# Running a gated linear recurrence inside the attention loop instead of ahead of it

## The chip, the cores and the metric

One Trainium2 chip, all 8 cores; each core computes one element of a batch of 8. The metric is the device time of the slowest core in microseconds (us). Before the change the kernel took 5171.43 us (median of 4 runs, 5058.72 to 5303.1; the two of them in the fast state, explained next, took 5059 and 5064).

Runs come in two states. In the fast one all cores end within about 1% of each other. In the slow one the cores of one die, or a pair of them, show a lower granted clock for part of the run, and the time is some per cent longer. Only fast runs, or cores that were not slowed, are compared here. In the profile, PE is TensorE, PEld its weight loads, ACT ScalarE, DVE VectorE, POOL GpSimd, SP SyncE (SPq its queue of transfers).

## The reference

One layer of a hybrid backbone: 4096 latent tokens and 256 context tokens of width 1024. Two mixers read the same normalised input; a SwiGLU block follows. Cut to what matters:

```python
# mixer A: bidirectional gated linear recurrence, width 1280
r = sigmoid(blockdiag(xc) @ wa + ba);  i = sigmoid(blockdiag(xc) @ wx + bx)
log_a = -8 * r * softplus(-lam);       a = exp(log_a)
b = sqrt(-expm1(2 * log_a)) * (i * xc)
h = scan(a, b) forward + scan(a, b) backward
ya = (h * gelu(g)) @ w_out_lru
# mixer B: attention, 8 query heads, 2 key heads, head size 128, 4096 queries x 4352 keys
yb = softmax(q @ k.T / sqrt(128)) @ v @ w_out_attn
x = x + g_m * ((sigmoid(ga) * ya + sigmoid(gb) * yb) @ w_out)     # then x + g_f * swiglu(...)
```

Nothing in mixer A needs mixer B before the two are joined, so the two may run at once.

## The kernel before

Its stages are modulation, input projections (A), recurrence (B), attention with the output projections of each tile of 512 queries (C), feed-forward (D). B, with cuts marked:

```python
for m in range(10):                       # 128 channels each
    for d in range(2):                    # two directions
        ab, a2 = abuf[d], a2buf[d]        # two decay buffers of 128 x 4352
        for (c0, n) in wtiles:            # 256, then 4 x 1024 columns
            ...                           # gate products: 2 gates x 2 or 3 weight chunks
            act(trt, psum_a, AF.Tanh);  act(ab[:, c0:c0+n], trt, AF.Exp)
            tt("pool", a2[:, c0:c0+n], ab[...], ab[...], ALU.mult)
            act(ti[:, c0:c0+n], psum_x, AF.Tanh)
        act(a2, a2, AF.Sqrt, scale=-0.25, bias=0.25)      # one pass over 4352 columns
        stt(ti, ti, 1.0, x32, ALU.add, ALU.mult)
        tt("dve", a2, a2, ti, ALU.mult)
        scan(...)
```

and the loop of C, 8 tiles x 8 heads x 17 pairs of key blocks:

```python
emit_S(0); emit_S(1)                      # query-key products of two iterations ahead
for i in range(len(items)):
    emit_rest(i)                          # exp, then 4 products: 2 with V, 2 with ones (the denominators)
    if i + 2 < len(items): emit_S(i + 2)
# in emit_rest, at a head's end (pr == 16):
    recip(rd, pd); tt("dve", att[h], po, rd, ALU.mult)    # VectorE reads the denominators from PSUM
```

After each tile, C also makes its output projections and converts one eighth of the feed-forward weights to bf16 for D; the transfers and casts of that lie beside the attention.

## Time and profile before

| stage of a fast core | us |
|---|---|
| modulation and A | 1358 |
| B, recurrence | 742 |
| C, attention, output projections, weight conversion | 1922 |
| D, feed-forward | 1034 |

The table of busy time by stage and the timelines are shown in the prediction. Here are three groups of instructions of core 0, which ended as in a fast run; the columns are line, engine, operation, output and inputs, shape, count, then busy time and mean ns of one, then the engine's idle time just before them and what ended most of it.

```profile
L309 ACT ACTIVATE pt<-psq 128x1024 bf16<-128x1024 f32 x1088 | 1112.9, 1023 | 731.6 <-PE psq L312 731.3
L312 PE MATMUL psq<-pt,Vt 128*128 128x512 bf16 x2176 | 820.7, 377 | 9.6 <-ACT pt L309 8.1
L312 PE MATMUL psq<-xcb,gw 128*128 128x512 bf16 (+1 forms) x936 | 298.6, 488 | 406.1 <-ACT tib L309 167.1 <-POOL gw L341 149.5 <-ACT trt L309 62.7
```

The attention's exponentials on ScalarE leave 732 us in which ScalarE waits for TensorE, while TensorE's products with V wait 10 us: TensorE bounds C. In B TensorE waits 406 us ahead of its 299 us of gate products. This is what invites the change.

### The profile page before, as it was taken

The page shows a single profiled execution, that of the slowest core. Times are in us where ns is not written, and L with a number is a line of the kernel's source. Part 1 is how long each engine was busy: PE and PEld are TensorE (multiplying, and loading weights), DVE is VectorE, ACT ScalarE, POOL GpSimd, SP SyncE. Part 2 cuts the span into 40 slices and gives each one's busy share as a digit, 9 for nine tenths or more (in the row PEclk, how much of TensorE's full clock was granted, in tenths as well). Part 3 has the DMA queues.
Part 4 walks back from the last instruction along what each step waited for, and adds up shares of the span by engine and source line. Part 5 has one row for each costly group of instructions (what it writes and reads, how often), then busy time and mean ns, then how long its engine had stood idle before and what let it go on. Part 6 is the DMA issues. An engine that isn't in the chain of part 4 may idle for free.

```text
span 5277.8 us, 55043 instructions; the slowest of 8 cores (5055.7 to 5277.8 us)
## 1 busy us (share of the span) xinstructions
PE 4418.2 (84%) x18234; PEld 1935.7 (37%) x18234; DVE 1599.1 (30%) x1353; ACT 2424.5 (46%) x3049; POOL 1223.2 (23%) x788
## 2 busy tenths in 40 slices
PE   8778777778444442999999999999999899999999
PEld 8533333333111110333333333333343344444444
DVE  0244444444366776121212222121212111111111
ACT  0455555555466554747474655746363211111111
POOL 2133333333366664210102021110101000000000
PEclk9999898899666675999999999998887777787889
DMA  9522122222222221621203030221210411111011
GB/s 300 166 81 81 64 85 83 83 83 73 92 95 91 89 89 56 193 84 45 98 20 114 9 109 28 90 74 46 76 33 17 167 48 48 48 48 48 30 43 37
DMA packets 208453, 417.75 MB, mean 79 GB/s; under 512 B 18416, under 2 KB 123376, under 8 KB 199728
## 3 DMA queue, kind: packets, MB, share of 16 engines
q1 hardware_dynamic: 208176, 414.23, 23.2%
q8 instruction: 153, 2.51, 0.2%
q14 instruction: 124, 1.02, 0.1%
HBM read 279.28 MB, written 134.87 MB: 78 GB/s over the span
## 4 chain that ended last, share of the span: by engine, by line
PE 64%; POOL 9%; DMA 8%; ACT 8%; issue 5%; DVE 5%; SPq 1%; ACTq 0%; DVEq 0%; POOLq 0%
PE psq L312 62%; POOL a2buf L318 5%; DMA TBd<-to 2%; DMA TA<-to 2%; POOL gw L341 2%; DMA XC<-xco 2%; ACT abuf L309 1%; PE psq L315 1%; POOL g L318 1%; POOL t L318 1%; ACT a2buf L309 1%; ACT L309 1%; ACT trt L309 1%; DVE xco L327 1%; ACT tib L309 1%
## 5 line engine op out<-in xcount | busy, mean ns | idle before, releaser
L309 ACT ACTIVATE pt<-psq 128x1024 bf16<-128x1024 f32 x1088 | 1115.0, 1025 | 788.4 <-PE psq L312 788.2
L312 PE MATMUL psq<-pt,Vt 128*128 128x512 bf16 x2176 | 848.2, 390 | 8.8 <-ACT pt L309 7.5
L312 PE MATMUL psq<-pt,onesb 128*128 128x512 bf16 x2176 | 849.6, 390 | 0.0
L312 PE MATMUL psq<-hT,wi 128*128 128x512 bf16 (+1 forms) x3040 | 698.4, 388 | 129.5 <-ACT ub L309 94.4
L312 PE MATMUL psq<-hfT,wfi 128*128 128x512 bf16 x2816 | 717.5, 426 | 0.0
L312 PE MATMUL psq<-qt,KT 128*128 128x512 bf16 x2176 | 672.0, 392 | 13.9 <-DMA qt<-Q 11.0
L312 PE MATMUL psq<-xcb,gw 128*128 128x512 bf16 (+1 forms) x936 | 291.0, 477 | 425.2 <-ACT tib L309 174.5
L330 DVE RECIPROCAL rden<-psq 128x512 f32<-128x512 f32 x64 | 214.9, 3358 | 1322.0 <-PE psq L312 1322.0
L312 PEld LDWEIGHTS psq<-hT,wi 128*128 128x128 bf16 x3040 | 300.2, 100 | 531.5 <-issue 231.8
L312 PEld LDWEIGHTS psq<-hfT,wfi 128*128 128x128 bf16 x2816 | 300.9, 107 | 413.2 <-issue 354.8
L318 POOL TENSOR_TENSOR a2buf<-abuf 128x1024 f32<-128x1024 f32 (+1 forms) x100 | 348.7, 3487 | 238.8 <-ACT abuf L309 238.8
L312 PEld LDWEIGHTS psq<-pt,Vt 128*128 128x128 bf16 x2176 | 211.5, 97 | 522.3 <-issue 418.3
L309 ACT ACTIVATE sg<-psq 128x512 f32<-128x512 f32 x176 | 105.3, 598 | 573.5 <-PE psq L312 573.4
L318 POOL TENSOR_TENSOR mt<-tmpc,mB 128x512 bf16<-128x512 f32 x64 | 80.9, 1265 | 1238.5 <-DVE tmpc L327 1238.5
L312 PE MATMUL psq<-wfo,aT 128*128 128x512 bf16 x1408 | 356.0, 423 | 0.0
L318 POOL TENSOR_TENSOR x1l<-tmpd,x1l 128x512 f32<-128x512 f32 x64 | 81.2, 1269 | 1107.6 <-DVE tmpd L318 936.0
L312 PEld LDWEIGHTS psq<-xcb,gw 128*128 128x128 bf16 x936 | 104.2, 118 | 611.5 <-issue 563.2
L312 PEld LDWEIGHTS psq<-qt,KT 128*128 128x128 bf16 x2176 | 217.5, 100 | 290.8 <-issue 88.2
L318 DVE TENSOR_TENSOR aT<-sg,psq 128x512 bf16<-128x512 f32 x176 | 121.1, 688 | 659.1 <-PE psq L312 645.2
L327 DVE SCALAR_TENSOR_TENSOR xco<-ub,pp,xco 128x512 f32<-128x512 f32 (+3 forms) x270 | 198.4, 755 | 278.8 <-ACT ub L309 204.7
L312 PEld LDWEIGHTS psq<-pt,onesb 128*128 128x128 bf16 x2176 | 214.8, 99 | 155.6 <-issue 36.2
L312 PEld LDWEIGHTS psq<-wfo,aT 128*128 128x128 bf16 x1408 | 149.7, 106 | 205.0 <-issue 167.0
(101 smaller groups left out, 4430.5 us busy)
## 6 DMA issues: line engine op xcount, KB each, us to landing
wm<-w_mod SPq DMA_DIRECT2D x12, 2048.0 KB, 12.0
stg<-w_in SPq DMA_DIRECT2D x24, 1024.0 KB, 14.6
xc<-XC SPq DMA_DIRECT2D x10, 2176.0 KB, 12.3
stgc<-w_ffn_in SPq DMA_DIRECT2D x40, 512.0 KB, 4.2
xt<-x SPq DMA_DIRECT2D x32, 512.0 KB, 6.5
xtc<-x SPq DMA_DIRECT2D x32, 512.0 KB, 9.8
X<-xtc SPq DMA_DIRECT2D x32, 512.0 KB, 2.8
xs<-X SPq DMA_DIRECT2D x32, 512.0 KB, 5.3
```

The costliest lines, as they stand in the source:

```text
L309: return S.add("act", lambda e: e.activation(out=out, in_=in_, func=func, **kw), reads, writes)
L312: return S.add("pe", lambda e: e.matmul(out, lhsT=lhsT, rhs=rhs, start=start, stop=stop), reads, writes)
L315: return S.add("pe", lambda e: e.transpose(out=out, in_=in_, identity=ident), reads, writes)
L318: return S.add(eng, lambda e: e.tensor_tensor(out=out, in0=in0, in1=in1, op=op), reads, writes)
L327: return S.add("dve", lambda e: e.scalar_tensor_tensor(out=out, in0=in0, scalar=scalar, in1=in1, op0=op0, op1=op1), reads, writes)
L330: return S.add("dve", lambda e: e.reciprocal(out=out, in_=in_), reads, writes)
L341: return S.add(eng, lambda e: e.tensor_copy(out=out, in_=in_), reads, writes)
```

## The change

Its intent is to fill TensorE's and ScalarE's idle time. The recurrence becomes a Python generator that emits one small step (256 columns instead of 1024) at a time, and the attention loop takes a step every 2.3 iterations. The buffers of both have to fit together, so the decay buffers go from two to one, the gates get a single PSUM bank, and the denominators one instead of two. VectorE would hold that bank for a reciprocal of 3.36 us, so ScalarE now copies the denominators out first. The output projections and the weight conversion no longer fit and move to a stage of their own after the attention, which goes through a new DRAM buffer.

```diff
+        def lru_steps():
+            for m in range(10):
 ...
+                    for t_ in range(NT):                       # 17 steps of 256 columns
+                        for gate in range(2):
+                            for ki, k in enumerate(ks):
+                                mm(psG.t[:, gate * 256:(gate + 1) * 256], ...)
+                        def gate_acts(...):                    # emitted two iterations later
+                            act(trt, psG[0:256], AF.Tanh); act(ti, psG[256:512], AF.Tanh)
+                            act(ab, trt, AF.Exp); tt("pool", a2, ab, ab, ALU.mult)
+                        pend.append([it[0], gate_acts])
+                        yield
+                    stt(...); act(a2, a2, AF.Sqrt, ...)
+                    yield
+                    tt("dve", a2, a2, ti, ALU.mult)
+                    yield
+                    scan(...)
+                    yield
+                    yield
 ...
             for i in range(len(items)):
                 emit_rest(i)
                 if i + 2 < len(items): emit_S(i + 2)
+                lru_pump()                                     # 0.44 steps per iteration
 ...
-                    recip(rd, pd); tt("dve", att[h], po, rd, ALU.mult)
+                    act(pds, pd, AF.Copy)                      # ScalarE, out of PSUM
+                    recip(rdb, pds); tt("dve", ato, po, rdb, ALU.mult)
+                    dma("sp", AT_d[h, tile], ato)
 ...
+        # new stage: loads of AT, Z, gates, x; output projections; weight conversion
```

## The prediction

> **What bounds the kernel now.** I read the spans of the cores first. The profiled run is a slow one; cores 0, 1, 6 and 7 ended at 5056 to 5070 us, as the two fast timed runs (5058.7, 5063.5) did, while cores 2 to 5 took 5243 to 5278. So core 0 stands for a fast run here, and every number below is of core 0 unless I say otherwise. Then I read one table of busy time by stage: modulation (to 204), input projections A (to 1358), gated recurrence B (to 2100), attention with output projections C (to 4022), feed-forward D (to the end).
>
> ```profile
> core 0: us, PE busy (x) PEld busy (x) DVE busy (x) ACT busy (x) POOL busy (x), PEclk, DMA share, GB/s
> 204.00:1358.00 1154.00, 1015.83 (x3748) 441.50 (x3746) 508.52 (x623) 659.50 (x1229) 389.55 (x328) 0.77 0.23 80
> 1358.00:2100.00 742.00, 298.55 (x936) 106.62 (x936) 495.29 (x90) 415.49 (x359) 447.87 (x140) 0.64 0.23 83
> 2100.00:4022.00 1922.00, 1861.91 (x8208) 730.46 (x8208) 393.70 (x328) 1115.41 (x1091) 258.37 (x224) 0.99 0.22 73
> 4022.00:5056.00 1034.00, 978.44 (x4496) 458.46 (x4496) 197.58 (x288) 213.39 (x330) 81.61 (x64) 0.96 0.19 66
> ```
>
> In B nothing is full: PE is busy 299 of 742 us, and the chain of waits goes through GpSimd squares, weight casts and scans. In C PE is full and VectorE and GpSimd are nearly idle. The change runs B inside C's attention loop, to fill one with the other.
>
> How tight is that loop? The timeline of ScalarE in it:
>
> ```profile
> 2127.42 1.02 ACT L309 ACTIVATE pt<-psq 128x1024 bf16<-128x1024 f32 x1 [0.71 <-PE psq L312]
> 2128.72 1.02 ACT L309 ACTIVATE pt<-psq 128x1024 bf16<-128x1024 f32 x1 [0.27 <-PE psq L312]
> 2130.14 1.02 ACT L309 ACTIVATE pt<-psq 128x1024 bf16<-128x1024 f32 x1 [0.40 <-PE psq L312]
> 2131.44 1.02 ACT L309 ACTIVATE pt<-psq 128x1024 bf16<-128x1024 f32 x1 [0.27 <-PE psq L312]
> ```
>
> Two exponentials take 2.72 us, 1.36 an iteration. PE's six 512-column matmuls start 0.2158 us apart (57 of them take 12.46 us in the projection that follows, the last one 0.38), so they need 1.295. The loop keeps two score tiles in flight, so its period is a round trip over two iterations: exponential 1.02, hand-over to PE 0.15, six matmuls 1.295, drain and hand-back 0.25, together 2.72. PE has only 0.065 us of slack in an iteration; ScalarE, whose back-to-back exponentials start 0.93 apart, has 0.43.
>
> What the recurrence costs ScalarE shows in the timeline of B:
>
> ```profile
> 1399.02 1.09 ACT L309 ACTIVATE tib<-psq,lc 128x1024 f32<-128x1024 f32 x1
> 1401.23 1.28 ACT L309 ACT_TABLE_LOAD   x1 [1.11 <-POOL a2buf L318]
> 1402.52 3.83 ACT L309 ACTIVATE a2buf<-a2buf 128x4352 f32<-128x4352 f32 x1
> 1406.37 1.28 ACT L309 ACT_TABLE_LOAD   x1
> 1407.67 0.47 ACT L309 ACTIVATE trt<-psq,lc 128x256 f32<-128x256 f32 x1
> 1408.23 0.60 ACT L309 ACTIVATE abuf<-trt,lc 128x256 f32<-128x256 f32 x1
> 1408.74 0.45 ACT L309 ACTIVATE tib<-psq,lc 128x256 f32<-128x256 f32 x1
> ```
>
> The square root waits 1.1 us for GpSimd's last square, then takes a table load, 3.83 us and a load back: ScalarE does nothing else for 7.5 us.
>
> [...] 1.28 us, two loads at each square root, none between tanh and exp. So putting tanh beside the attention's exp is free of loads; the 20 square roots are not. [...] after 8 us of idle at the start of C,
>
> ```profile
> 2119.32 1.86 PE L312 MATMUL psq<-qt,KT 128*128 128x512 bf16 x4 [8.06 <-DMA qt<-Q]
> ...
> 2123.25 0.63 PE L312 MATMUL psq<-pt,onesb 128*128 128x512 bf16 x1
> 2123.68 0.63 PE L312 MATMUL psq<-pt,Vt 128*128 128x512 bf16 x1
> 2124.11 0.63 PE L312 MATMUL psq<-pt,onesb 128*128 128x512 bf16 x1
> ```
>
> matmuls start 0.43 us apart until 2126.2, then 0.216. [...] The cap is in the trace, 0.81[...]: cores 0 and 1 have it from 204 to about 1500 us and again from about 1600 to 1700, while cores 2 and 3 of the same die don't; they and cores 4 and 5 get it from 3590 to 3800 on, for about 1300 us, in the midst of dense work. That is the slow state. [...] With all eight cores running the trace shows 304 GB/s in the first 100 us at a DMA share of 0.97; I use 300.
>
> **The change, part by part.** Stages up to 1358 us and D (1034 us) are not touched. In place of B and C (2664 us) stand a fused stage and a projection stage.
>
> Fused stage. (a) Head: keys, values and the first queries are loaded as at the start of C now, where PE waited some 20 us: 22. (b) The loop alone: 8 tiles x 136 iterations x 1.36 = 1480. (c) Gate steps: 10 x 2 x 17 = 340 of 256 columns, one in every 2.3 iterations. On PE each is 2 gates x 2.6 weight chunks x 0.11 (half of 0.216) = 0.57 us, put between the scores and the next value matmuls. PE's slack is 0.065, so nearly all of it lengthens the round trip: 340 x 0.58 = 197, taking the slack as lost to ScalarE's uneven load. Its ScalarE work is two tanh and one exp, 0.47 + 0.45 + 0.60 less two overlaps of 0.09, 1.3 us every 2.3 iterations, against a slack there of 2.3 x 0.43 + 0.57 = 1.56: it fits on average, barely. (d) Square roots: 20 x 7.5 = 150, all on the path, since ScalarE runs in order and the next exponential stands behind. (e) PE is idle over 8 us at each, goes to half clock and comes back after 5 us, in which two iterations run instead of 3.7: 20 x 2.3 = 46. (f) The denominators now have one PSUM bank, and ScalarE copies it out at the end of each of 64 heads. That copy waits for the last ones-matmul, so the next exponential starts 1.86 us after the last one's end instead of 0.34. Part of these 1.5 us comes back from the slack: 64 x 1.1 = 70. (g) The pipeline drains at 8 tile ends: 10. (h) The cap still holds when the loop now starts at 1380: to 1500 and 1600 to 1700, 220 us at 0.81[...]: 25. Sum: 22 + 1480 + 197 + 150 + 46 + 70 + 10 + 25 = 2000.
>
> VectorE (495 us of recurrence, and 64 x (3.36 + 0.69) for the heads) and GpSimd (under 450) fit easily in 2000. The scheduling leaves four empty steps after a square root, about 24 us, for multiply, product and scan (5.4 + 4.7 + 9.4); I take the single decay buffer's wait as hidden.
>
> Projection stage. PE work is 8 x 208 matmuls x 0.216 = 360, with the end of a tile about 47 us each. But the traffic that the attention hid is now here: weights 26 x 0.5 MB = 13.6 MB, 8 tiles x (6.4 MB in, 2.1 MB out) = 68, conversion of the feed-forward weights 35 MB in and 17 out = 52; 134 MB at 300 GB/s is 445 us. The transfers are issued in order by one queue: loads of the next tile 22 us, nine conversions 24, stores of the tile 8, a cycle of 54 against PE's 47. With a first tile that waits for weights (about 70) the stage takes 70 + 7 x 54 + 22 = 470.
>
> Total: 1358 + 2000 + 470 + 1034 = 4862; rounded 4870. Against 5060 in the fast state that is 3.8% less. Of B's 742 us, 194 are won.
>
> **The rivals.** R1, full overlap: ScalarE or PE saturate and nothing else counts. PE alone needs 1088 x 1.295 + 340 x 0.57 = 1603; ScalarE 1088 x 0.93 + 340 x 1.3 + 20 x 7.5 + 64 x 0.5 = 1636. Then the fused stage is about 1680 and the projections, PE-bound with the first load, 400: 4470. Against it: the queue between the two engines is only two tiles deep, so a stall of one cannot be caught up by the other. R2, waits in order: a decay buffer or the one gate bank is not free when ScalarE comes to it; in B a square on GpSimd took 9.3 us beside a scan and 1.9 without. If each of 20 scans holds ScalarE 8 us more, and each of these cools PE, 200 are added: 5070, no gain. For it: buffers go from two to one. Against: the empty steps were made for it. R3, the clock: cores capped late are then capped in D and part of the projections, +150 to +200, the slow state as before; or a cap that starts in the fused stage stretches it to 2250: 5110. R4, the projection stage runs at 230 GB/s, the share seen where 1 KB rows were loaded (2100 to 2200): 134 MB is 580, and the total 4980.
>
> **Range and chances.** The big terms, gate steps, square roots with cold clock, and DMA-bound projections, each may be off by 70 us; R1 pulls down, R2 and R4 up. I take 4870 with 4720 to 5040 as the eight-in-ten range. Faster by over 2% means below 4960: 0.80. Same: 0.15. Slower: 0.05.
>
> **What would show it.** In the fused stage: iterations without a gate step at 1.36 us, with one about 0.5 more; 20 gaps of PE of 8 us that end at a square root, then 0.43 us spacing; exponentials after a copy that start 1.9 us after the one before ended. A fused stage under 1800 or over 2200 makes step (c) or (d) wrong; exponentials waiting for VectorE would be R2. In the projections: a DMA share of 0.9 or more and PE waiting for loads; if PE is full and the tile takes 47 us, the traffic was hidden. Stage A and D must be unchanged, or the difference is the cap's.

## The result

The changed kernel takes 4909.98 us (median of 11 runs; fast runs 4899 to 4943), the kernel before 5063.54 in the same rounds. The ratio is 0.9699 with a 95% interval of 0.968 to 0.9719: 3% faster. A ratio is the mean time of one kernel's fast runs over that of the other's fast runs of the same rounds, so it is not quite the ratio of the medians. The results are correct.

Busy time by stage, on the slowest core of a fast run (columns: the window, its length, busy us and count of PE, PEld, DVE, ACT, POOL, then TensorE's granted clock, the DMA share and GB/s). The rows are A, the fused stage, the projection stage and D:

```profile
0.00:1358.00 1358.00, 1058.17 (x4594) 573.84 (x4594) 512.46 (x647) 675.91 (x1269) 435.79 (x360) 0.91 0.33 108
1358.00:3357.00 1999.00, 1703.73 (x8296) 789.97 (x8296) 678.72 (x208) 1636.99 (x2233) 407.44 (x390) 0.95 0.12 42
3357.00:3879.40 522.40, 382.02 (x1680) 168.88 (x1680) 143.52 (x213) 71.43 (x72) 175.53 (x141) 0.86 0.79 259
3879.40:4913.00 1033.60, 976.61 (x4496) 456.21 (x4496) 202.32 (x288) 213.25 (x330) 82.47 (x64) 0.96 0.19 66
```

A and D did not move. B and C together, 2664 us, became 1999 + 522 = 2521. In the fused stage neither engine is full, 1704 and 1637 of 1999, though together they hold more work than before. The page's groups answer to those of before:

```profile
L310 ACT ACTIVATE pt<-psq 128x1024 bf16<-128x1024 f32 x1088 | 1098.2, 1027 | 252.2 <-PE psq L313 239.5
L313 PE MATMUL psq<-pt,Vt 128*128 128x512 bf16 x2176 | 844.4, 388 | 263.2 <-ACT pt L310 256.9
L313 PE MATMUL psq<-xcb,gw 128*128 128x256 bf16 x1768 | 249.1, 273 | 0.0
```

ScalarE's wait for TensorE fell from 732 to 252 us, TensorE's wait for ScalarE rose from 10 to 263, and no idle time stands ahead of the gate products. In total the two engines now wait for each other about as long, but not at the same places: of TensorE's 263 us, 148 are the 20 square roots and 75 come right after the copies of the denominators.

Where gate steps fall close together, ScalarE's timeline reads (start, duration, engine, line, operation, idle before it if any):

```profile
1643.27 2.15 ACT L310 ACTIVATE pt<-psq 128x1024 bf16<-128x1024 f32 x2
1645.31 0.47 ACT L310 ACTIVATE trt<-psq,lc 128x256 f32<-128x256 f32 x1
1645.67 0.48 ACT L310 ACTIVATE tib<-psq,lc 128x256 f32<-128x256 f32 x1
1646.02 0.61 ACT L310 ACTIVATE abuf<-trt,lc 128x256 f32<-128x256 f32 x1
1646.51 2.14 ACT L310 ACTIVATE pt<-psq 128x1024 bf16<-128x1024 f32 x2
```

and TensorE's gate products beside it:

```profile
1640.88 0.82 PE L313 MATMUL psq<-xcb,gw 128*128 128x256 bf16 x6
...
1644.13 0.82 PE L313 MATMUL psq<-xcb,gw 128*128 128x256 bf16 x6
```

Two iterations with one gate step take 3.24 us (1643.27 to 1646.51) on ScalarE, where the view shows no idle time, and 3.25 on TensorE, also with none (2 x 1.295 for the attention's products and 6 x 0.109 for the gates make 3.24). TensorE is full here, and ScalarE nearly so: the view leaves out gaps under 0.15 us, and in the trace with one gate chunk (below) most of these pairs of iterations take ScalarE 3.04. Where a gate step has four products instead of six, TensorE needs 3.03 too. The trace has 470 to 480 ns for a tanh of 256 columns, and 0.36 us from the first tanh to the second. In the kernel before, a tanh takes 1102 ns on 1024 columns and 473 on 256; from these two I estimate 0.82 ns a column, so that more than half of the 473 ns is a fixed part.

### The profile page after: what moved, and what is told of

It is laid out like the page before. It is cut to its first block, busy times and chain, and to the rows that moved or that the text cites. A ratio compares the mean times of both kernels' runs of the same rounds, so it can differ in the third digit from the quotient of the medians.

```text
span 4912.8 us, 59039 instructions; the slowest of 8 cores (4868.6 to 4912.8 us)
## 1 busy us (share of the span) xinstructions
PE 4120.5 (84%) x19066; PEld 1988.9 (40%) x19066; DVE 1537.0 (31%) x1356; ACT 2597.6 (53%) x3903; POOL 1101.2 (22%) x955
## 4 chain that ended last, share of the span: by engine, by line
PE 57%; DMA 16%; ACT 10%; issue 6%; DVE 5%; SPq 3%; POOL 2%; ACTq 0%; DVEq 0%; POOLq 0%
PE psq L313 55%; ACT pt L310 4%; SPq L307 3%; DMA TBd<-to 2%; DMA TA<-to 2%; DMA WFI<-cvo 2%; DMA XC<-xco 2%; DMA X<-xtc 2%; ACT a2buf L310 1%; DMA stgc<-w_ffn_in 1%; PE psq L316 1%; DMA GG<-hgo 1%; POOL t L319 1%; POOL g L319 1%; ACT L310 1%
## 5 line engine op out<-in xcount | busy, mean ns | idle before, releaser
L310 ACT ACTIVATE pt<-psq 128x1024 bf16<-128x1024 f32 x1088 | 1098.2, 1027 | 252.2 <-PE psq L313 239.5
L313 PE MATMUL psq<-hfT,wfi 128*128 128x512 bf16 x2816 | 609.1, 379 | 0.0
L331 DVE RECIPROCAL rden<-pds 128x512 f32<-128x512 f32 x64 | 214.4, 3350 | 1020.2 <-ACT pds L310 1020.2
L319 POOL TENSOR_TENSOR a2buf<-abuf 128x256 f32<-128x256 f32 x340 | 226.9, 668 | 1328.1 <-ACT abuf L310 1328.1
L313 PEld LDWEIGHTS psq<-hfT,wfi 128*128 128x128 bf16 x2816 | 275.5, 98 | 330.5 <-issue 0.3
L313 PE MATMUL psq<-wfo,aT 128*128 128x512 bf16 x1408 | 305.2, 379 | 0.0
L310 ACT ACTIVATE cvo<-stgc 128x1024 bf16<-128x1024 f32 x70 | 70.2, 1007 | 361.1 <-DMA stgc<-w_ffn_in 273.8
L313 PE MATMUL psq<-xcb,gw 128*128 128x256 bf16 x1768 | 249.1, 273 | 0.0
L310 ACT ACTIVATE abuf<-trt,lc 128x256 f32<-128x256 f32 x340 | 207.8, 611 | 13.2 <-DVE tib L334 13.2
L313 PEld LDWEIGHTS psq<-xcb,gw 128*128 128x128 bf16 x1768 | 173.3, 98 | 93.4 <-issue 1.1
```

Of the source, the lines that this page charges most:

```text
L310: return S.add("act", lambda e: e.activation(out=out, in_=in_, func=func, **kw), reads, writes)
L313: return S.add("pe", lambda e: e.matmul(out, lhsT=lhsT, rhs=rhs, start=start, stop=stop), reads, writes)
L319: return S.add(eng, lambda e: e.tensor_tensor(out=out, in0=in0, in1=in1, op=op), reads, writes)
L331: return S.add("dve", lambda e: e.reciprocal(out=out, in_=in_), reads, writes)
```

## The experiments

"Loop" below is the time from the first query-key product to the start of the last copy of the denominators, on a core at full clock. In the changed kernel the core profiled above gives 3351.10 - 1384.11 = 1967 us; two other cores gave 1964 and 1965. The projection stage is from that copy to the first load of D: 528 on that core, 520 and 525 on the two others. The ranges in the table are of two or three cores each; over all eight cores of the changed kernel the loop is 1964 to 1968 and the projection stage 520 to 536.

| run | loop, us | projection stage, us | fast runs, us | ratio to before |
|---|---|---|---|---|
| changed kernel | 1964 to 1967 | 520 to 528 | 4910 | 0.9699 |
| copy later | 1916 (two cores at full clock) | 521 to 525 | 4855 (one) | none |
| root on VectorE (wrong) | 1914 | 522 to 530 | 4857 to 4863 | none |
| no table load (wrong) | 1910 | 525 to 526 | 4839 to 4856 | none |
| one gate chunk (wrong) | 1939 to 1940 | 525 to 529 | 4873, 4874, 4944 (two cores slowed for a part) | none |
| root gone (wrong) | 1829 to 1833 | 522 to 527 | 4767 to 4781 | 0.9427 |
| recurrence after the loop | 1581 | not read | 5770 (one) | none |
| conversion in the fused stage | 1969 | 453 to 457 | 4835 (one) | none |
| three edits | 1916 to 1917 | 431 to 436 | 4796 (one) | none |
| exp off (wrong) | 1909 to 1912 | 523 to 526 | 4849, 4860 | 0.9586 |
| exp off and one chunk (wrong) | 1820 | 519 to 533 | 4759, 4764 | 0.9402 |
| conversion issued by ScalarE | 1964 to 1966 | 555 to 569 | 4939 (one) | none |
| three edits again | 1913 to 1918 | 431 to 439 | 4759 to 4763 | 0.9398 |

Where there is no ratio, too few fast runs of one of the two kernels came together.

### The denominators' copy later

```diff
-                    pds = pdsR.next(); act(pds, pd, AF.Copy); recip(...); tt(...); dma(...)
+                    tails.append(tail)     # the same five lines, as a function
...                  # in the next emit_rest, right after its exp:
+                while tails: tails.pop(0)()
```

> Each head's tail (ScalarE's copy of the denominators out of PSUM, then VectorE's reciprocal and product) is emitted after the next head's first exponential instead of before it; same results. Theory (my term f: the copy stands on ScalarE ahead of the next head's exponential, and TensorE waits for that): the fused stage loses 64 x 0.8 to 1.1, so 50 to 70 us, and the total goes from 4910 to 4840 to 4860. Rival (the copy only fills time in which ScalarE waits for TensorE, which packs the loop): under 15 us, no verdict but same.

Its one fast run took 4855, and an undisturbed die in a slow run had its cores at 4823 to 4844, against 4869 to 4913 for the changed kernel: some 50 us less. The profiled run was slow, but its cores 4 and 5 were not slowed in the loop (mean granted clock 0.953 there, as in the changed kernel): it took 1916 us on both, 50 less than 1964 to 1967. The version with three edits, which has this one, agrees: 1916 against the 1969 of the version that differs by this edit in the loop. The theory holds. The timeline of ScalarE at a head's end, first of the changed kernel, then of the version with three edits:

```profile
3326.46 0.60 ACT L310 ACTIVATE pds<-psq 128x512 f32<-128x512 f32 x1 [1.26 <-PE psq L313]
3326.95 1.93 ACT L310 ACTIVATE pt<-psq 128x1024 bf16<-128x1024 f32 x2
```

```profile
1729.74 1.03 ACT L310 ACTIVATE pt<-psq 128x1024 bf16<-128x1024 f32 x1
1730.65 0.61 ACT L310 ACTIVATE pds<-psq 128x512 f32<-128x512 f32 x1
1731.12 1.05 ACT L310 ACTIVATE pt<-psq 128x1024 bf16<-128x1024 f32 x1
```

Before, ScalarE sat 1.26 us until the head's last denominator product was done, although the next head's exponential was ready. After, the copy stands between two exponentials and no time is lost.

### The square root: moved, without its tables, and gone

Three kernels, all wrong:

```diff
-  act(a2, a2, AF.Sqrt, scale=-0.25, bias=0.25)
+  ts("dve", a2, a2, -0.25, 0.25, ALU.mult, ALU.add); ts1("dve", a2, a2, 0.5, ALU.max)   # root on VectorE
+  act(a2, a2, AF.Copy, scale=0.25)                                                      # no table load
+  act(a2[:, 0:8], a2[:, 0:8], AF.Copy, scale=0.25)                                      # root gone
```

No run has a true root on VectorE (a power of 0.5); the maximum stands in its place.

> Wrong result on purpose: the square root of the recurrence leaves ScalarE, and two VectorE passes of the same size (one with a maximum in place of the root) take its place. Theory (terms d and e, the roots with their two table loads stop the exponentials, and TensorE comes back cold): the fused stage loses up to 196 us, 20 x (7.5 + 2.3), and the total is 4715 to 4750. Rival (the longer chain on VectorE makes ScalarE wait for the gate buffers instead, or the exponentials' lead of two iterations hides part of the root): less than 120 us. A cross-check: table loads in the fused stage fall from over 40 to a handful.

> Wrong result on purpose: the square root on ScalarE is replaced by a copy with a scale on the same elements, which needs no other table; the pass of about 3.8 us stays, the two table loads of 1.28 us each around it go. Theory: ScalarE's stop per root goes from 7.5 to about 4.9, so 20 x 2.6 = 51 us less, total about 4860. Rival (the stop is filled from queued exponentials anyway): under 20 us. Together with the run that takes the whole root away it gives the part of the pass and of the cold clock: if the clock's part (46 us) is real, the whole root is worth much more than 51 + 20 x 3.8 = 127 us.

> Wrong result on purpose: the root's pass over 4352 columns becomes a copy of 8 columns on ScalarE, so no table load, no long pass, and no pass added to VectorE. The run that moved the root to VectorE gained only 52 us of the fused stage, while ScalarE's waits of the gate step on VectorE's chain grew from 13 to 123 us. Theory (the root is worth about 160, the 52 were what the new wait left): here that wait stays near 13 us and the fused stage falls from 1966 to 1790 to 1825, total 4735 to 4770. Rival (my terms d and e were too large by more than half; the root's long pass hides behind queued work): the fused stage stays above 1880, total above 4820.

Without tables (the fused stage has 40 table loads in the changed kernel and none in each of these three) the loop lost 56 us; 40 table loads last 40 x 1.28 = 51. With the root moved to VectorE it lost 52, no more. Taken alone that would say that the long pass costs nothing. The waits say otherwise. The rows have engine, line, what was waited for, then total us, times and longest; the changed kernel, the root on VectorE, the root gone:

```profile
ACT abuf L310 <- DVE tib L334: 13.2, 3, 5.8
```

```profile
ACT abuf L310 <- DVE tib L334: 93.6, 10, 12.7
ACT abuf L310 <- DVE xc L334: 29.7, 9, 6.1
```

```profile
ACT abuf L310 <- DVE tib L334: 35.9, 10, 5.9
```

Two more passes on VectorE before each scan made the single decay buffer come free later, and ScalarE, which keeps to the order of its program (as in the 1.26 us ahead of the copy, above), stood 123 us instead of 13 before the gate's exponential, with the attention's exponentials behind it. So that experiment put a new wait in place of the one that it took away. With the root gone and VectorE left as it was, the loop fell by 134 us, to 1829 to 1833. That is a little outside the expected 1790 to 1825, and far from the rival's 1880. One part of that expectation missed: the wait was to stay near 13 us and rose to 36 (the last row above), so the 134 are not the whole price.

All these traces have the same 1088 exponentials in the same order, so the distances from one to the next can be compared one by one (core 3 of the changed kernel, core 2 of the root gone). The 20 distances that hold a root are 125 us shorter in sum; those after a root, up to the next gate step, are 39 us shorter; those of that gate step are 25 us longer, by the new wait; the others together are 5 us longer. So a root costs at two places, 164 us in all. The first is the stop itself: without tables it is 54 us shorter (40 loads of 1.28 us are 51), and the long pass is the other 71. The second is TensorE's cold clock. After one root, the changed kernel first, then the root gone:

```profile
2343.48 0.59 PE L313 MATMUL psq<-pt,Vt 128*128 128x512 bf16 x1 [7.67 <-ACT pt L310]
...
2346.29 1.02 ACT L310 ACTIVATE pt<-psq 128x1024 bf16<-128x1024 f32 x1 [2.05 <-PE psq L313]
```

```profile
2275.91 0.38 PE L313 MATMUL psq<-pt,Vt 128*128 128x512 bf16 x1 [1.40 <-ACT pt L310]
...
2277.46 1.03 ACT L310 ACTIVATE pt<-psq 128x1024 bf16<-128x1024 f32 x1 [0.78 <-PE psq L313]
```

TensorE has been idle for 7.67 us, and its next products start 0.43 us apart instead of 0.216, so six of them take some 1.27 us longer; ScalarE waits 2.05 us for them instead of 0.78. In the 9 us after a root TensorE's granted clock is 0.63 on average over the 20 roots, with the root gone 0.99. Without tables, where ScalarE still stops for the pass, it is 0.73, and this second part stays within about 1 us of the changed kernel's. In the run with the root on VectorE both parts go as well (183 us), but the gate steps after the roots lose 112 to the new wait and the others 18: 52 are left.

### The gate step: each engine's part, and both

```diff
-                            for ki, k in enumerate(ks):
+                            for ki, k in enumerate(ks[:1]):           # one gate chunk: 680 products, not 1768
```
```diff
-                            act(ab, trt, AF.Exp, scale=..., bias=...)
+                            cast("pool", ab, trt)                     # exp off: GpSimd copies instead
```

Their outputs are wrong, which doesn't matter for the times.

> Wrong result on purpose: each gate product uses only its first weight chunk, 4 or 2 gate matmuls... exactly two per step of 256 columns in place of four to six; ScalarE's work is unchanged. Theory (term c: where a gate step falls, TensorE is packed and its matmuls of 0.109 us lengthen the iteration): about 3.2 matmuls fewer x 0.109 x 340 steps = 119 us, total about 4790. Rival (ScalarE's three small activations are what a gate step costs, TensorE's part hides): under 40 us.

> Wrong result on purpose: the gate step's exponential on ScalarE becomes a copy on GpSimd; TensorE's work is unchanged. In the trace of the changed kernel two iterations with one gate step take ScalarE 2 x 1.02 + 0.36 + 0.36 + 0.49 = 3.25 us from start to start, and TensorE 2 x 1.295 + 6 x 0.109 = 3.24: both are full. Theory (both bind at once, so taking work from one alone gives little): of 340 x 0.49 = 167 us taken from ScalarE only 20 to 60 are gained, fused stage 1905 to 1945. Rival (ScalarE alone binds, and the fewer gate products gave little for that reason): 130 to 167 gained, fused stage 1800 to 1835.

> Wrong result on purpose: both at once, one weight chunk per gate product and the gate's exponential on GpSimd. Theory (both engines bind where a gate step falls): the two together give clearly more than the sum of each alone (27 and some 40): 110 to 150 us, fused stage 1815 to 1855. Rival (something else sets the pace, such as the lead of two iterations or the wait on buffers): no more than the sum, fused stage above 1890.

One chunk took 1088 x 0.109 = 119 us from TensorE and gained 27. The exponential took 167 from ScalarE and gained 56. Both together gained 146, clearly more than 27 + 56 = 83. The pairs of iterations with one gate step (201 without a root or a copy in each trace) show why. In the changed kernel 106 of them take about 3.2 us, TensorE's time for six products, and 86 take 3.0 to 3.1. With one chunk 183 take 3.0 to 3.1: that is what ScalarE needs, so no more could be gained. With the exponential off 114 still take 3.2. With both, 170 take 2.8. The exponential was not taken away here but moved to GpSimd. No new wait of ScalarE or TensorE shows for it, but ScalarE's 13 us of waiting for the decay buffer are gone (GpSimd now waits for it, 58 us), so up to 13 of the 56 may be that. The first run alone met the number of its rival, "ScalarE's part is what a gate step costs", but the second run shows that the rival's reason is wrong too: it would have gained 130 to 167. ScalarE's timeline without the exponential:

```profile
1644.26 0.47 ACT L310 ACTIVATE trt<-psq,lc 128x256 f32<-128x256 f32 x1
...
1645.29 1.02 ACT L310 ACTIVATE pt<-psq 128x1024 bf16<-128x1024 f32 x1 [0.20 <-PE psq L313]
1646.58 1.02 ACT L310 ACTIVATE pt<-psq 128x1024 bf16<-128x1024 f32 x1 [0.27 <-PE psq L313]
1647.51 0.47 ACT L310 ACTIVATE trt<-psq,lc 128x256 f32<-128x256 f32 x1
```

From gate step to gate step it is still 3.25 us, and the 0.49 us that ScalarE saved now shows as two waits for TensorE, 0.20 and 0.27. With one chunk as well, the same distance in a like place was 2.85 us (1646.32 to 1649.17). The two engines, one full and the other within a tenth of it (3.24 and 3.04 us), hid each other's savings here: 27 and 56 us alone, 146 together.

### The recurrence after the loop

```diff
-            if j == 0: lru_pump(1)
-                lru_pump()                 # in the loop; the whole recurrence is emitted after it
```

> The recurrence is taken out of the attention's loop and emitted after it; same results. Theory (terms b, f, g): the attention loop alone takes 22 + 1480 + 70 = about 1575 us from its first product, then the recurrence takes some 500 us alone, as in the kernel before. The fused stage's 1966 less this loop is what the recurrence still costs inside it: my sum says 197 + 150 + 46 = 393. Rival (the loop itself is slower than 1.36 us an iteration, and the recurrence is nearly hidden): the loop alone takes over 1700.

Busy time by stage, first the loop alone, then the recurrence alone:

```profile
1371.80:2953.00 1581.20, 1488.90 (x6528) 566.11 (x6528) 254.82 (x126) 1138.19 (x1152) 0.00 (x0) 1.00 0.03 11
2953.00:4153.00 1200.00, 431.38 (x1768) 209.28 (x1768) 427.55 (x82) 577.97 (x1080) 428.17 (x390) 0.50 0.14 51
```

The loop alone takes 1581, as the theory said (1575). In it 1024 distances between exponentials without a copy are 1.37 us on average and 63 with a copy 2.79, so the period is right and the copies cost 63 x 1.42 = 90 us, not 70. So the recurrence costs 1967 - 1581 = 386 us inside it, where my sum had 393. The expectation of "some 500 us alone" missed: in this form, with one gate bank, one decay buffer and steps of 256 columns, the recurrence alone takes 1200 us, longer than the 742 of the kernel before. Its parts wait for each other in a row: TensorE's bursts of six gate products take 1.44 us with gaps of 1.08 us between them where I read the timeline, and its granted clock is 0.50 over the 1200 us. What is slow alone is cheap as filler: of 1200 us, 386 are paid.

### The projection stage

```diff
# conversion in the fused stage: a piece of 512 columns per 8 iterations (the denominators' copy has one buffer, to make room)
+  if ph == 0: dma("sp", cvs, src)
+  if ph == 3: cast("pool", cvo, cvs)
+  if ph == 6: dma("sp", dst, cvo)
# conversion issued by ScalarE, in the projection stage
-  dma("sp", stg, src); ...; dma("sp", dst, co)
+  dma("act", stg, src); ...; dma("act", dst, co)
# three edits: copy later + conversion in the fused stage + the broadcast row first
+  make_row(gmh, ...)                       # now ahead of the weight loads and casts
```

> The conversion of the feed-forward weights (132 pieces of 512 columns) moves from the projection stage into the fused stage, one piece per 8 iterations, its cast from ScalarE to GpSimd; same results. Theory (the projection stage's cycle of 60 us is the chain of transfers, TensorE needs 47): the projection stage goes from 525 to about 74 + 8 x 47 = 450, at most 470, the fused stage stays within 10 us, total about 4835. Rival (TensorE's own pace and its late start set the stage): projection stage above 500. Rival (the transfers disturb the fused stage): the fused stage grows by over 30.

> The weight conversion's transfers in the projection stage are issued from ScalarE's queue instead of SyncE's; same results, same bytes. Theory (the 60 us cycle is issue and waiting in order on one queue: loads of the next tile stand behind conversions that wait for buffers): the cycle falls to 47 to 53 us and the projection stage to 460 to 490. Rival (bandwidth or the transfers' own latency sets it, whoever issues): the stage stays at 510 to 530.

> Three correct edits together: the head's tail after the next head's first exponential (gave about 50 us), the weight conversion in the fused stage (expected 75), and the broadcast row of the projection stage computed before the weight casts, so that TensorE starts some 50 us earlier there. If they add up: fused stage about 1915, projection stage 400 to 440, total 4730 to 4780, 3% under the changed kernel. If the projection stage waits for its weights anyway, the third gives nothing: about 4785 to 4800.

> The version with the three correct edits again, for an interval, since three of its four runs fell in the slow state: fast runs at 4755 to 4800, ratio to the kernel before 0.938 to 0.95.

The queue's timeline gives the cycle of a tile as the distance between the loads of `att`; in the changed kernel, then with the conversion moved:

```profile
3604.98 0.43 SPq L307 DMA_DIRECT2D att<-AT  x1
3664.03 0.37 SPq L307 DMA_DIRECT2D att<-AT  x1
```

```profile
3608.59 0.43 SPq L307 DMA_DIRECT2D att<-AT  x1
3654.48 0.43 SPq L307 DMA_DIRECT2D att<-AT  x1
```

The cycle falls from some 60 us (59 here, then 60) to 45.9, which is TensorE's own pace (208 products x 0.216 = 45), the stage from 520 to 528 down to 453 to 457, and the loop does not notice (1969 against 1967). So the conversion set the projection stage's pace, and the fused stage had room for it. Issuing the conversions from ScalarE's queue made the stage longer, 555 to 569, which neither expectation had (460 to 490, 510 to 530). So taking them off SyncE's queue does not help by itself; but on ScalarE each load still stands in order, behind casts and stores (casts wait 407 us for their loads there, 361 in the changed kernel), so the run does not show that the order is harmless. Whether that, the transfers' rate or the time from a transfer to its cast and back sets the cycle, these runs do not tell apart; in the changed kernel the stage's mean was 259 GB/s at a DMA share of 0.79, below the 302 at 0.98 of the 70 us from 3360 to 3430, near its start.

In the changed kernel TensorE's first projection started 80 us into this stage: the row that it broadcasts needs VectorE, which had to do the weight casts first. With the row first, and the other two edits, the stage takes 431 to 439, so the earlier start gave about 20 us. TensorE's first projection then came 19 to 20 us into the stage, but it waits for the weights there. The three edits add up, in both runs of this version.

It is correct and in the second run takes 4759 to 4763 in four fast executions, 0.9398 of the kernel before (0.9383 to 0.9413). That is 0.9398 / 0.9699 = 0.969 of the changed kernel, by the two ratios to the same kernel. It is the fastest correct version here.

## Why the prediction was right

The time predicted was 4870, the median measured 4910, inside the range. By its own steps:

| step | predicted, us | measured, us | from |
|---|---|---|---|
| A | 1358 | 1358 | stage table |
| (a) head of the fused stage | 22 | 26 | 1358 to the first product |
| (b) loop, (f) copies, (g) drains | 1480 + 70 + 10 = 1560 | 1581 | recurrence after the loop |
| (c) gate steps | 197 | 209 | 386 less the next two rows |
| (d) roots | 150 | 138 | root gone: 125, and 13 of waiting for GpSimd's last square, which that kernel keeps |
| (e) cold clock | 46 | 39 | root gone, distances after a root |
| (h) clock cap | 25 | 0 | no time at 0.81 in the changed kernel's trace |
| end | 0 | 6 | last copy to 3357 |
| fused stage | 2000 | 1999 | stage table |
| projection stage | 470 | 522 | stage table |
| D | 1034 | 1034 | stage table |

The fused stage came out at the very number. That is luck in part: the steps are off by 4 to 25 us each, with both signs, and cancel. But each is near its size. Step (b), the period of 1.36 us, is right: exponentials without a gate step between are 1.29 and 1.43 us apart in the changed kernel too. The copies (f) were sized at 70 and cost 90 in the loop alone; moving them gave some 50 back. The roots (d) and the cold clock (e) are there as the prediction said, 138 and 39 us for 150 and 46. In the changed kernel TensorE was idle for 6.0 to 8.6 us at the 20 roots and its products then ran at half speed for 2.5 to 6.3 us, 4.5 on average; step (e) had over 8 and 5. Step (h) was read from a slow run's cores; in the fast run profiled for the changed kernel the clock records of all eight cores have no time at 0.81. Its 25 us were my estimate: in the slow run an iteration took 1.575 us at 0.81 (core 4, from 3700 us on) and 1.36 at 1.00 (core 0).

Step (c) has the right size with half of the reason. Its 209 us are 0.61 a step (279 gate steps have no root or copy in their two or three iterations; these take 0.61 more than 1.36 each, on average a step), and it said 0.58. But it put that cost on TensorE alone and said that ScalarE's work "fits on average, barely". Taking TensorE's share away gives 27 us, not 119, because ScalarE alone then needs 3.04 us for two iterations with a gate step, more than the 2.72 that two without one take.

The term that made the total 40 to 50 us too small is the projection stage, +52. The step counted a cycle of 54 us a tile; it was 60, and 70 + 7 x 60 + 22 = 512, so the cycle makes 42 of the 52. In the cycle from 3604.98 to 3664.03 the conversions hold the queue for 34 us where the step had 24, the loads for 15 where it had 22. The late start of TensorE behind the casts on VectorE was not in the sum; with the conversion moved it is worth 20 us, and what it costs in the changed kernel was not tested. That the traffic of the conversion sets this stage and not TensorE was right, as the moved conversion shows, though the DMA share was 0.79 and not the 0.9 that was to show it.

Of the rivals, R1 (full overlap, 4470) fell: the engines wait for each other 240 to 257 us each in the fused stage. R2 (waits on buffers) was nearly absent, 13 us, but it was real as a danger: it came back with 123 us as soon as VectorE got two more passes, and with 36 when the root went. R3 described the slow runs only (5170, 5238 here). R4 (230 GB/s, 580 us) lay on the right side for the projection stage, but too far.

## What to carry to other kernels

When two stages are run as one, add the busy time of each engine for the smallest repeated piece, here two iterations with one gate step, and look for engines that are full, or nearly, at the same place: cutting work on one of them alone then gives little (27 and 56 us here), on both it gives more than the sum (146). Work with slack, like the weight conversion (some 70 us off the projection stage here, and 2 on the loop), is best kept where the bound is another engine, and everything that stands in order on an engine's queue (a copy at a head's end, a small row ahead of casts; some 50 and 20 us here) should be placed by when its input is ready. An experiment that moves work to another engine measures the move, not the work; take it away to price it, and compare the waits even then, or a new one hides part of the price (134 us of 164 here).
